# A two-block decoder layer on one core: the order of the delta rule's steps and the engines of its small operations

## The chip, the cores and the metric

The kernel runs on one core of a Trainium2 chip. The core has five engines that work side by side, each through its own instructions in order: TensorE (PE; its weight loads are shown apart as PEld), VectorE (DVE), ScalarE (ACT), GpSimd (POOL) and SyncE (SP), which here only issues DMAs. The metric is the device time of one execution, in microseconds (us), as the median of several runs.

## The reference

Two transformer blocks over one sequence of 256 tokens, width 1024, in float32. The first has two mixers side by side, forgetting attention and a gated delta rule, whose outputs are gated, added and projected, and an MLP with squared ReLU; the second has a SwiGLU, a token mixer and another SwiGLU. What the change touches is the delta rule, with 8 heads of width 128 and chunks of 64 tokens, and a detail of the MLP:

```python
def first_block(x, ...):
    u = rmsnorm(x, norm_mix_g[l])
    proj = u @ w_in[l]
    ...
    qkv = jax.nn.silu(causal_depthwise_conv(jnp.concatenate([gq, gk, gv], axis=-1), gdn_conv_w[l]))
    ...
    o_a = gated_delta_rule_chunked(qh, kh, vh, g, beta).transpose(0, 2, 1, 3)
    o_a = rmsnorm(o_a, gdn_norm_g[l]) * jax.nn.silu(z)
    ...
    x = h + jnp.square(jax.nn.relu(hn @ w_up[l])) @ w_down[l]

def gated_delta_rule_chunked(q, k, v, g, beta):
    ...
    kk = jnp.einsum('bhncd,bhnsd->bhncs', k, k)
    a_mat = jnp.where(tri_strict, beta[..., None] * kk * decay, 0.0)
    rhs = jnp.concatenate([v * beta[..., None], k * (beta * jnp.exp(G))[..., None]], axis=-1)
    sol = lax.linalg.triangular_solve(a_full, rhs, left_side=True, lower=True, unit_diagonal=True)
    ...
    def step(s, inp):
        v_new = value_c - jnp.einsum('bhcd,bhde->bhce', kcum_c, s)
        o = (jnp.einsum('bhcd,bhde->bhce', qdec_c, s)
             + jnp.einsum('bhcs,bhse->bhce', attn_c, v_new))
        s = s * dec_c[..., None, None] + jnp.einsum('bhcd,bhce->bhde', kdec_c, v_new)
        return s, o
```

## The kernel before

**Main line.** The matrix products of both blocks follow each other as one long row of products for TensorE, here called main products: a 128x128 piece of a weight against 256 tokens. `Feed` streams the weights: SP fetches 2048 columns at a time into `raw` (L203, three buffers), ScalarE casts 1024 of them to `wh` (L220), VectorE subtracts to get the rest `wl` (L221), and each piece is used in three products (L258 to L260; L349 to L351 in the projections of the first block's end). A pair `wh`, `wl` feeds 24 main products. Products over 256 columns follow each other at 0.11 to 0.12 us.

**Side lines.** Everything else, norms, attention, the delta rule, runs in generators that `Lines` steps between main products: each `yield pe, wait` says how much TensorE time a stage took and how long, by estimate, until the next may follow. A scheduler then fixes one order for each engine. The order is static: an instruction that is not ready holds everything behind it on its engine.

**The delta rule.** The 8 heads are worked in four groups of two, and two groups form a `Pair` (groups 0 and 1, then 2 and 3). `gdn_group` does for each group:

- the decays: a row DMA on GpSimd's queue with a mask (`rows_everywhere`, L619, L621), exponentials on ScalarE (L755);
- the products of k with k and q (L766); VectorE makes from them `bm`, the matrix to be solved (L780), and `at` (L783);
- `pair.load`: `bm` is written to DRAM as an image (L685) and its diagonal blocks come back (`blk`, L693), both on SP's queue, in order with the `raw` loads;
- `rsqrt_cols` on GpSimd: a bit trick and three Newton rounds on four columns (L146 to L154), then the factor of v (L790);
- the transposes of v and their scaling into `vt` (L798, L801 by way of L170 on ScalarE), then transposes of q and k with squares and scalings (L810 to L816);
- the solution. When both groups of a pair are loaded, `Pair.solve` runs 31 steps of forward substitution on GpSimd for all blocks (L709, L713) and writes to `solved` in DRAM (L716). Each group then fetches its half (`packed` in the tile `xp`, L824, a DMA of GpSimd's queue) and spreads it over four 32-column blocks of `tt` (L833, two on ScalarE, two on VectorE);
- products that finish the inverse (`pp` L849, `pu` L856) and the recurrence (L871 to L911, `apply`), with short VectorE and ScalarE steps between; `HOP` is the wait given between them;
- the output's norm: squares on ScalarE (L919), the sum and the root on GpSimd (L923, `rsqrt_cols`), the scaling of `bm` (by way of L170), the final transposes (L932).

L170 is the helper `scale_rows`, so rows of it are told apart by their tiles. The end of the last two groups falls into the projections of the first block, whose `gate` additions run on GpSimd (L1153). Later, in the MLP, `operand` lays out the second product's operands `ah` and `al` with 4 and 60 unused columns in front (L1174, L1175); the SwiGLUs use 0.

## Time and profile before

| what | us |
|---|---|
| median of 3 runs (lowest, highest) | 1048.19 (1047.76, 1049.74) |
| the profiled execution's own time | 1044.6 |
| its span in the profile | 1042.8 |
| TensorE busy in it | 1005.7 |
| VectorE busy | 673.5 |
| ScalarE busy | 557.0 |
| GpSimd busy | 262.6 |

The profile shows one execution, instruction by instruction; its times count from the start of the span. A row of a timeline gives an instruction's start, its length, its line and operation, its tiles, and in brackets how long the engine had been idle before it and what ended that. The granted clock is TensorE's, as a share of 2.4 GHz: 1.00 is the upper level, 0.50 the lower, 1.2 GHz. Some records of products are missing from a trace, a few in a hundred at most.

### The profile page before, as it was taken

What the parts mean: (1) busy time and instruction counts of PE and PEld (TensorE: products, weight loads), DVE (VectorE), ACT (ScalarE), POOL (GpSimd) and SP (SyncE); (2) the same over time, 40 slices, a digit from 0 to 9 for tenths busy, and PEclk for the clock granted to TensorE, in tenths of its full rate; (3) what the DMA queues carried; (4) which work ended last, traced back from release to release, by engine and by line L of the source; (5) the groups of instructions that cost most, each with busy time, mean ns of one, the idle gap of its engine ahead of it and who ended that gap; (6) DMA issues with size and microseconds to landing.
All of it is one profiled execution on the core that took longest, in us unless ns stands there. A gap on an engine that the chain in (4) does not pass through costs nothing. (4 is left out here: it accounts for less than half of the span.)

```text
span 1042.8 us, 20129 instructions
## 1 busy us (share of the span) xinstructions
PE 1005.7 (96%) x8126; PEld 976.3 (94%) x8126; DVE 673.5 (65%) x1070; ACT 557.0 (53%) x1000; POOL 262.6 (25%) x509
## 2 busy tenths in 40 slices
PE   8999999699797999999999999999999999999997
PEld 7888999699797999999999999999989899999996
DVE  6676898475474787664555666576775687666453
ACT  6766766254634556554444444445576755444542
POOL 1358167638405110000010211140004511121000
PEclk9999999899898999999999999999999999999998
DMA  8656366454342365555455555467644445554551
GB/s 292 242 169 216 123 187 183 146 157 148 92 147 97 119 215 192 183 182 200 167 200 169 196 178 186 152 215 232 220 154 162 163 133 212 187 197 165 167 191 45
DMA packets 39117, 181.93 MB, mean 174 GB/s; under 512 B 11936, under 2 KB 14128, under 8 KB 21232
## 3 DMA queue, kind: packets, MB, share of 16 engines
q1 hardware_dynamic: 37344, 174.85, 48.6%
q0 software_dynamic: 1248, 5.27, 1.9%
q8 instruction: 63, 1.03, 0.4%
q10 hardware_dynamic: 432, 0.53, 0.1%
q14 instruction: 30, 0.25, 0.1%
HBM read 178.25 MB, written 2.38 MB: 173 GB/s over the span
## 5 line engine op out<-in xcount | busy, mean ns | idle before, releaser
L221 DVE TENSOR_TENSOR wl<-raw,wh 128x1024 fp32r<-128x1024 f32 (+2 forms) x347 | 418.2, 1209 | 230.7 <-ACT wh L220 219.7
L220 ACT CAST wh<-raw 128x1024 fp32r<-128x1024 f32 (+2 forms) x347 | 343.8, 996 | 339.4 <-PE g L259 300.6
L259 PE MATMUL g<-Bl,wh 128*128 128x256 f32 x816 | 227.5, 279 | 0.0
L260 PE MATMUL g<-Bh,wl 128*128 128x256 f32 x816 | 227.1, 279 | 0.0
L258 PE MATMUL g<-Bh,wh 128*128 128x256 f32 x816 | 226.9, 279 | 0.0
L258 PE MATMUL g<-Ah,wh 128*128 128x256 f32 x776 | 219.5, 284 | 0.3 <-DVE fnat L994 0.3
L260 PE MATMUL g<-Ah,wl 128*128 128x256 f32 x776 | 219.7, 284 | 0.0
L259 PE MATMUL g<-Al,wh 128*128 128x256 f32 x776 | 218.9, 283 | 0.0
L260 PE MATMUL g<-ah,wl 128*128 128x256 f32 x608 | 170.4, 280 | 0.7 <-DVE wl L221 0.7
L258 PE MATMUL g<-ah,wh 128*128 128x256 f32 x608 | 170.6, 281 | 0.0
L259 PE MATMUL g<-al,wh 128*128 128x256 f32 x608 | 170.6, 281 | 0.0
L258 PEld LDWEIGHTS g<-Bh,wh 128*128 128x128 f32 x816 | 154.3, 190 | 0.0
L260 PEld LDWEIGHTS g<-Bh,wl 128*128 128x128 f32 x816 | 153.3, 188 | 0.0
L259 PEld LDWEIGHTS g<-Bl,wh 128*128 128x128 f32 x816 | 153.3, 188 | 0.0
L258 PEld LDWEIGHTS g<-Ah,wh 128*128 128x128 f32 x776 | 147.7, 191 | 0.9 <-DVE fnat L994 0.7
L259 PEld LDWEIGHTS g<-Al,wh 128*128 128x128 f32 x776 | 146.9, 189 | 0.2
L260 PEld LDWEIGHTS g<-Ah,wl 128*128 128x128 f32 x776 | 146.9, 189 | 0.1
L260 PEld LDWEIGHTS g<-ah,wl 128*128 128x128 f32 x608 | 114.8, 189 | 0.9 <-DVE wl L221 0.9
L258 PEld LDWEIGHTS g<-ah,wh 128*128 128x128 f32 x608 | 114.7, 189 | 0.0
L259 PEld LDWEIGHTS g<-al,wh 128*128 128x128 f32 x608 | 114.7, 189 | 0.0
L1211 POOL TENSOR_TENSOR s<-s,row 128x512 f32<-128x512 f32 x22 | 37.7, 1714 | 207.6 <-ACT s L1210 207.6
L427 POOL TENSOR_TENSOR acc<-acc,sq 128x512 f32<-128x512 f32 x10 | 14.1, 1411 | 243.9 <-ACT sq L422 243.9
(323 smaller groups left out, 1413.4 us busy)
## 6 DMA issues: line engine op xcount, KB each, us to landing
raw<-in_w_in_dram SPq DMA_DIRECT2D x44, 1024.0 KB, 4.9
raw<-in_ffn_gu_dram SPq DMA_DIRECT2D x44, 1024.0 KB, 4.8
raw<-in_ffn_dn_dram SPq DMA_DIRECT2D x32, 704.0 KB, 4.1
raw<-in_w_up_dram SPq DMA_DIRECT2D x16, 1024.0 KB, 4.8
raw<-in_w_down_dram SPq DMA_DIRECT2D x16, 1024.0 KB, 4.8
raw<-in_w_out_dram SPq DMA_DIRECT2D x8, 1024.0 KB, 4.8
raw<-in_w_proj_fox_dram SPq DMA_DIRECT2D x4, 1024.0 KB, 4.7
raw<-in_w_proj_gdn_dram SPq DMA_DIRECT2D x4, 1024.0 KB, 4.7
```

Of the source, the lines that this page charges most:

```text
L220: nc.scalar.copy(hi[:, r], raw[:, r])
L221: nc.vector.tensor_tensor(out=lo[:, r], in0=raw[:, r], in1=hi.bitcast(F32)[:, r], op=ALU.subtract)
L258: nc.tensor.matmul(out, lhsT=w_h, rhs=xh[:, k, :], start=(k == 0), stop=False)
L259: nc.tensor.matmul(out, lhsT=w_h, rhs=xl[:, k, :], start=False, stop=False)
L260: nc.tensor.matmul(out, lhsT=w_l, rhs=xh[:, k, :], start=False, stop=(k == nk - 1))
L427: e.tensor_tensor(out=acc, in0=acc, in1=sq, op=ALU.add)
L1211: nc.gpsimd.tensor_tensor(out=s, in0=s, in1=u.row2, op=ALU.mult)
```

## The change

- A new function `gdn_decays` makes the decays of all four groups; it is spawned for each before the groups, and a group takes its decays from there.
- v is transposed and scaled behind the `pu` product instead of before the solution; the transposes of q and k, with squares and scalings, stand behind the spreading of the solution. The squares' unused output goes to `vnew` instead of `uu`.
- `Pair.solve` itself fetches the packed solutions of both groups, right behind the write, into one tile `packed` that takes the buffer of `sol`.
- Two memsets of each group move from GpSimd to VectorE, and so do the output's sum and root.
- The waits given to the generators change: `HOP` 2.1 for 2.5, 4 for 3 in the solve, 5.5 for 8 in front of the final transposes.
- `ah` and `al` start at offset 0.

```diff
         if jj % 4 == 3:
-            yield 0.0, 3.0
+            yield 0.0, 4.0
         gp.dma_start(out=out.rearrange("a (n i) c -> (a n) (i c)", n=4), in_=sol.rearrange("p i c -> p (i c)"))
+        yield 0.0, 4.0
         self.solved = True
-        yield 0.0, 6.0
+
+        self.packed = g.gx.tile([P, 2, P], F32, tag="sol", name=nm(g, "packed"))
+        for par in range(2):
+            gp.dma_start(
+                out=self.packed[:, par].rearrange("p (a c) -> p a c", c=8),
+                in_=out[16 * par : 16 * par + 16].rearrange("a p c -> p a c"),
+            )
+        yield 0.0, 7.0
         self.done = True
+
+def gdn_decays(g, grp):
+    par, h0 = grp % 2, 2 * grp
+    dec = g.gx.tile([P, 4, P], F32, tag=f"at{par}", name=nm(g, "at"), bufs=2)
+    rows_everywhere(g, dec.rearrange("p (h c) n -> p h (c n)", h=2), h0, 1, g.con["mgdn"], slice(0, 2))
+    yield 0.0, 7.0
+    ngc = g.ngc[:, h0 : h0 + 2].rearrange("p h c -> p (h c)")
+    for i in range(4):
+        g.nc.scalar.activation(out=dec[:, i], in_=dec[:, i], func=AF.Exp, bias=ngc[:, i : i + 1])
+    g.dec[grp] = dec
+    yield 0.0, 1.0
...
-    HOP = 2.5
+    HOP = 2.1
...
-    while "v" not in have:
-        yield 0.0, 0.3
-    vt = have["v"]
-    pv = bank()
-    for i, (h, c) in enumerate(inst):
-        nc.tensor.transpose(pv[:, i], vt[:, h, c * P : (c + 1) * P], g.ident)
-    vn = vt.rearrange("p h (c n) -> p (h c) n", c=2)
-    for i in range(4):
-        scale_rows(g, vn[:, i], pv[:, i], nkv[:, i : i + 1])
-    yield 0.45, 0.0
...
     while not pair.done:
         yield 0.0, 0.5
-    packed = xp[:, 0]
-    nc.gpsimd.dma_start(
-        out=packed.rearrange("p (a c) -> p a c", c=8), in_=pair.out[16 * par : 16 * par + 16].rearrange("a p c -> p a c")
-    )
-    yield 0.0, 7.0
+    packed = pair.packed[:, par]
...
-    nc.gpsimd.memset(half(xp, 1), 0.0)
-    yield 0.0, 3.5
+    nc.vector.memset(half(xp, 1), 0.0)
+
+    kdn = vnew[:, 1:4:2]
+    pk, pq = bank(), bank()
...
+    yield 0.66, 2.8
...
-    nc.gpsimd.memset(y[up], 0.0)
-    yield 0.9, HOP
+    nc.vector.memset(y[up], 0.0)
+    yield 0.9, 0.0
+
+    while "v" not in have:
+        yield 0.0, 0.3
+    vt = have["v"]
...
+    yield 0.45, HOP
...
-    gp.tensor_tensor(out=so, in0=so, in1=base, op=ALU.add)
-    rsqrt_cols(g, r2, so, f"rsq{par}")
+    nc.vector.tensor_tensor(out=so, in0=so, in1=base, op=ALU.add)
+    rsqrt_cols_on(g, nc.vector, r2, so, f"rsq{par}")
     for i in range(4):
         scale_rows(g, o[:, i], o[:, i], r2[:, i : i + 1])
-    yield 0.0, 8.0
+    yield 0.0, 5.5
...
-        ah = operand(act, nf, 4, "ah", "ah")
-        al = operand(act, nf, 60, "al", "al")
+        ah = operand(act, nf, 0, "ah", "ah")
+        al = operand(act, nf, 0, "al", "al")
```

How the order changes, at three places.

ScalarE before, between two weight casts of group 3's projections; `vt_1658` is v of group 2, `tt_1910` and `tt_1963` the spread solutions of groups 0 and 1:

```order
L220 CAST wh_2462<-raw_2408 128x1024
L170 ACTIVATE cacc_2333<-g_2258,par 128x256
L170 ACTIVATE vt_1658<-w_2426,cl_2089 128x128 x4
L220 CAST wh_2525<-raw_2523 128x1024
...
L220 CAST wh_2587<-raw_2585 128x1024
L1118 ACTIVATE gate_1589<-g_2461 128x512
L170 ACTIVATE tt_1910<-xp_1911,con 128x4x32 x2
L639 ACTIVATE kq_2175<-cacc_2340 128x256
L170 ACTIVATE tt_1963<-xp_1964,con 128x4x32 x2
L220 CAST wh_2659<-raw_2585 128x1024
```

And now; `vnew_1942` and `vnew_1967` take the squares of groups 0 and 1, `vt_966` and `vt_1285` are their v:

```order
L220 CAST wh_2704<-raw_2622 128x1024
L170 ACTIVATE tt_1940<-packed_2498,con 128x4x32 x2
L170 ACTIVATE tt_1965<-packed_2498,con 128x4x32 x2
L842 ACTIVATE vnew_1942,ss_1703<-w_2653 128x128 x4
L842 ACTIVATE vnew_1967,ss_1718<-w_2674 128x128 x3
L170 ACTIVATE vnew_1942<-w_2652,ed 128x128
L842 ACTIVATE vnew_1967,ss_1718<-w_2674 128x128
L220 CAST wh_2754<-raw_2752 128x1024
...
L220 CAST wh_2824<-raw_2752 128x1024
L170 ACTIVATE vt_966<-w_2784,cl_1704 128x128 x4
L170 ACTIVATE vt_1285<-w_2793,cl_1719 128x128 x4
```

The scaling of v left the place between the casts and follows the spreading; the spreading of both groups stands three casts later than before, together with the squares.

VectorE now, where the first pair's solution is spread; `bm_2301` is the matrix of group 3, whose image is the last input of the second solve:

```order
L799 SCALAR_TENSOR_TENSOR bm_2301<-w_2330,cl_2303,at_1617 128x128
L221 TENSOR_TENSOR wl_2705<-raw_2622,wh_2704 128x1024
L823 TENSOR_SCALAR tt_1940<-packed_2498,con 128x4x32
L802 TENSOR_TENSOR at_1617<-w_2330,at_1617 128x128
L799 SCALAR_TENSOR_TENSOR bm_2301<-w_2330,cl_2303,at_1617 128x128
L823 TENSOR_SCALAR tt_1940<-packed_2498,con 128x4x32
L823 TENSOR_SCALAR tt_1965<-packed_2498,con 128x4x32 x2
L802 TENSOR_TENSOR at_1617<-w_2330,at_1617 128x128
```

Before, all of group 3's `bm` stood well behind the spreading, among products of group 0; now its last scaling comes right behind the first `tt`.

GpSimd before, at the end of group 2; `gate` is the first block's gate, `so` and `r` the sum and root of the output's norm:

```order
L1153 TENSOR_TENSOR gate_1590<-gate_1590,zt_3905 128x512
L923 TENSOR_TENSOR so_3697<-so_3697,cl_2089 128x4
L146 TENSOR_SCALAR r_528_3743<-so_3697 128x4
L149 TENSOR_SCALAR rsq_3745<-so_3697 128x4
L151 TENSOR_TENSOR rsq_3745<-r_528_3743 128x4
L1153 TENSOR_TENSOR gate_1590<-gate_1590,zt_3943 128x512
L152 TENSOR_TENSOR rsq_3745<-rsq_3745 128x4
```

And VectorE now, with the same sum and root of group 2:

```order
L221 TENSOR_TENSOR wl_3880<-raw_3847,wh_3879 128x1024
L929 TENSOR_TENSOR bm_1943<-bm_1943,w_3656 128x2x128
L937 TENSOR_TENSOR so_3663<-so_3663,cl_1945 128x4
L146 TENSOR_SCALAR r_524_3703<-so_3663 128x4
L149 TENSOR_SCALAR rsq_3705<-so_3663 128x4
L151 TENSOR_TENSOR rsq_3705<-r_524_3703 128x4
L152 TENSOR_TENSOR rsq_3705<-rsq_3705 128x4
L1162 SCALAR_TENSOR_TENSOR gate_3309<-gate_3309,g_3806 128x512
L153 TENSOR_SCALAR rsq_3705<-rsq_3705 128x4
```

The root left GpSimd, where only the gate additions remain, and stands on VectorE between its weight subtractions. On TensorE the final transposes of groups 2 and 3 stand 64 and 42 main products behind their last product of the recurrence before, 99 to 104 and 102 now.

## Rows read from the trace of the kernel before

**Rows 1.** The page, section 1: busy time, share of the span, instructions by engine.

```profile
PE 1005.7 (96%) x8126; PEld 976.3 (94%) x8126; DVE 673.5 (65%) x1070; ACT 557.0 (53%) x1000; POOL 262.6 (25%) x509
```

**Rows 2.** Slices of 20 us: PE, PEld, DVE, ACT, POOL busy, clock, DMA share, GB/s.

```profile
180.00:200.00 20.00, 11.56 (x98) 11.28 (x97) 10.46 (x21) 7.61 (x16) 15.39 (x53) 0.85 0.33 89
200.00:220.00 20.00, 18.69 (x140) 18.11 (x139) 15.33 (x46) 9.21 (x16) 7.37 (x16) 0.90 0.52 169
...
240.00:260.00 20.00, 20.00 (x177) 20.00 (x176) 9.17 (x15) 9.74 (x29) 16.34 (x45) 1.00 0.45 159
260.00:280.00 20.00, 13.51 (x105) 13.30 (x104) 9.07 (x14) 12.26 (x39) 9.14 (x29) 0.83 0.27 66
...
320.00:340.00 20.00, 13.92 (x91) 12.40 (x90) 7.80 (x10) 9.26 (x26) 13.08 (x33) 0.83 0.27 100
340.00:360.00 20.00, 19.34 (x163) 18.92 (x163) 14.30 (x18) 7.75 (x10) 3.49 (x2) 1.00 0.29 106
```

**Rows 3.** The same table for the three stretches at half clock.

```profile
193.86:204.10 10.24, 4.81 (x18) 4.44 (x19) 6.54 (x14) 5.90 (x12) 6.31 (x17) 0.50 0.62 178
265.54:272.37 6.83, 3.20 (x15) 3.20 (x16) 3.87 (x8) 5.58 (x13) 4.01 (x13) 0.50 0.15 10
330.40:337.22 6.82, 5.32 (x23) 4.73 (x23) 2.63 (x3) 2.20 (x5) 5.14 (x14) 0.50 0.01 4
```

**Rows 4.** Waits of TensorE, 180 to 345: us in total, times, longest.

```profile
PE w L911 <- ACT vnew L170: 6.5, 1, 6.5
```

**Rows 5.** Timeline of ScalarE: start, us, instruction, idle before and its releaser.

```profile
195.24 1.14 ACT L170 ACTIVATE vt<-w,cl 128x128 f32<-128x128 f32 x4 [10.75 <-POOL cl L790]
...
208.47 0.93 ACT L170 ACTIVATE tt<-xp,con 128x128 f32<-128x128 f32 x2 [7.27 <-DMA xp<-solved]
...
336.48 1.28 ACT L170 ACTIVATE bm<-bm,r 128x128 f32<-128x128 f32 x4 [4.20 <-POOL r L154]
```

**Rows 6.** Timeline of TensorE in A.

```profile
199.29 1.65 PE L766 MATMUL w<-kq 128*128 128x256 f32 x3 [8.44 <-DVE kq L640]
```

**Rows 7.** Timeline of GpSimd in A, the write and the fetches.

```profile
196.84 0.65 POOL L716 DMA_DIRECT2D solved<-sol  x1 [0.30 <-POOL sol L713]
200.82 2.32 POOL L824 DMA_DIRECT2D xp<-solved  x2 [3.32 <-DMA solved<-sol]
```

**Rows 8.** Timeline of GpSimd, the second solve's first step, write and fetch.

```profile
230.48 0.24 POOL L709 TENSOR_TENSOR stmp<-blk,sol 128x31 f32<-128x31 f32 x1 [7.73 <-DMA blk<-img]
...
259.88 0.65 POOL L716 DMA_DIRECT2D solved<-sol  x1 [0.30 <-POOL sol L713]
262.52 1.20 POOL L824 DMA_DIRECT2D xp<-solved  x1 [1.99 <-DMA solved<-sol]
```

**Rows 9.** Timeline of GpSimd in C, a gate addition and a root's start.

```profile
315.87 1.26 POOL L1153 TENSOR_TENSOR gate<-gate,zt 128x512 f32<-128x512 f32 x1 [25.52 <-DVE zt L1152]
...
329.81 0.20 POOL L923 TENSOR_TENSOR so<-so,cl 128x4 f32<-128x4 f32 x1 [1.39 <-ACT at L919]
```

**Rows 10.** All instructions of L824, 180 to 280: time from issue to landing.

```profile
DMA to landing us min/median/max: 3.7/5.4/7.6
```

**Rows 11.** TensorE in three stretches: length, busy (instructions), clock, DMA share, GB/s.

```profile
463.00:555.00 92.00, 92.00 (x774) 1.00 0.52 184
570.00:697.00 127.00, 127.00 (x1081) 1.00 0.53 185
...
866.00:990.00 124.00, 124.00 (x1096) 1.00 0.53 182
```

**Rows 12.** Timeline of SP's queue, the last image.

```profile
219.79 0.38 SPq L685 DMA_DIRECT2D img<-bm  x1
```

**Rows 13.** VectorE by line and shape, 160 to 345: busy, mean ns, idle before.

```profile
L221 DVE TENSOR_TENSOR wl<-raw,wh 128x1024 fp32r<-128x1024 f32 x43 | 55.0, 1278 | 37.0 <-ACT wh L220 32.6 <-PE g L260 4.4
...
L777 DVE TENSOR_TENSOR cl<-cl,beta 128x2 f32<-128x2 f32 x4 | 0.8, 212 | 0.0
```

**Rows 14.** Timeline of VectorE in front of C.

```profile
316.00 2.22 DVE L221 TENSOR_TENSOR wl<-raw,wh 128x1024 fp32r<-128x1024 f32 x1 [0.28 <-ACT wh L220]
```

More of the change, by code (lines that the diff above doesn't have):

```diff
@@ L749, in gdn_group @@
     ed = g.ed[:, h0 : h0 + 2]
-    at = dec = buf("at", 2)
-    rows_everywhere(g, dec.rearrange("p (h c) n -> p h (c n)", h=2), h0, 1, g.con["mgdn"], slice(0, 2))
-    yield 0.0, 6.0
-    for i in range(4):
-        nc.scalar.activation(out=dec[:, i], in_=dec[:, i], func=AF.Exp, bias=ngc[:, i : i + 1])
+    while grp not in g.dec:
+        yield 0.0, 0.3
+    at = dec = g.dec[grp]
     bm = buf("bm", 2)
@@ L791, in gdn_group @@
     yield 0.0, 2.0
-    while "v" not in have:
-        yield 0.0, 0.3
-    vt = have["v"]
-    pv = bank()
-    for i, (h, c) in enumerate(inst):
-        nc.tensor.transpose(pv[:, i], vt[:, h, c * P : (c + 1) * P], g.ident)
-    vn = vt.rearrange("p h (c n) -> p (h c) n", c=2)
-    for i in range(4):
-        scale_rows(g, vn[:, i], pv[:, i], nkv[:, i : i + 1])
-    yield 0.45, 0.0
     while pair.before and grp - 2 not in pair.before.passed:
@@ L805, in gdn_group @@
     uu, tt, xp, vnew = (buf(n) for n in ("uu", "tt", "xp", "vnew"))
-    kdn = vnew[:, 1:4:2]
-    pk, pq = bank(), bank()
-    for i, (h, c) in enumerate(inst):
-        nc.tensor.transpose(pq[:, i], kq[:, 1, h, c * P : (c + 1) * P], g.ident)
-    for h in range(2):
-        nc.tensor.transpose(pk[:, h], kq[:, 0, h, 0:P], g.ident)
-    for i in range(4):
-        nc.scalar.activation(out=uu[:, i], in_=pq[:, i], func=AF.Square, accum_out=ss[:, 4 + i : 5 + i])
-    for h in range(2):
-        scale_rows(g, kdn[:, h], pk[:, h], ed[:, h : h + 1])
-    gp.tensor_scalar(out=base, in0=ss[:, 4:8], scalar1=P * EPS, scalar2=4 * P * EPS * EPS, op0=ALU.mult, op1=ALU.add)
-    yield 0.66, 0.0
     while not pair.done:
         yield 0.0, 0.5
-    packed = xp[:, 0]
-    nc.gpsimd.dma_start(
-        out=packed.rearrange("p (a c) -> p a c", c=8), in_=pair.out[16 * par : 16 * par + 16].rearrange("a p c -> p a c")
-    )
-    yield 0.0, 7.0
+    packed = pair.packed[:, par]
     for n in range(4):
@@ L841, in half @@
         return v[:, :, :, side]
-    nc.gpsimd.memset(half(xp, 1), 0.0)
-    yield 0.0, 3.5
+    nc.vector.memset(half(xp, 1), 0.0)
+    kdn = vnew[:, 1:4:2]
+    pk, pq = bank(), bank()
+    for i, (h, c) in enumerate(inst):
+        nc.tensor.transpose(pq[:, i], kq[:, 1, h, c * P : (c + 1) * P], g.ident)
+    for h in range(2):
+        nc.tensor.transpose(pk[:, h], kq[:, 0, h, 0:P], g.ident)
+    for i in range(4):
+        nc.scalar.activation(out=vnew[:, i], in_=pq[:, i], func=AF.Square, accum_out=ss[:, 4 + i : 5 + i])
+    for h in range(2):
+        scale_rows(g, kdn[:, h], pk[:, h], ed[:, h : h + 1])
+    gp.tensor_scalar(out=base, in0=ss[:, 4:8], scalar1=P * EPS, scalar2=4 * P * EPS * EPS, op0=ALU.mult, op1=ALU.add)
+    yield 0.66, 2.8
     mask = g.con["m32"].rearrange("p (n b) -> p n b", b=32)
@@ L859, in gdn_group @@
     y, st = xp[:, 0:2], xp[:, 2:4]
-    nc.gpsimd.memset(y[up], 0.0)
-    yield 0.9, HOP
+    nc.vector.memset(y[up], 0.0)
+    yield 0.9, 0.0
+    while "v" not in have:
+        yield 0.0, 0.3
+    vt = have["v"]
+    pv = bank()
+    for i, (h, c) in enumerate(inst):
+        nc.tensor.transpose(pv[:, i], vt[:, h, c * P : (c + 1) * P], g.ident)
+    vn = vt.rearrange("p h (c n) -> p (h c) n", c=2)
+    for i in range(4):
+        scale_rows(g, vn[:, i], pv[:, i], nkv[:, i : i + 1])
+    yield 0.45, HOP
     o = bm
@@ L1101, in first_block @@
         gates = [gp.tile([P, 4, T], F32, tag=f"gate{w}", name=f"gate{w}") for w in range(3)]
+        g.dec = {}
+        for i in range(4):
+            ln.spawn(gdn_decays(g, i), 0.4 * i)
         pairs = [Pair(g)]
```

## The prediction

> **What bounds the kernel now.** I read the page first: TensorE is busy 1005.7 us of a span of 1042.8 [rows 1], so 37 us are idle. The change edits the delta rule, so I cut the stretch that holds it into slices of 20 us [rows 2]: from 240 to 260 TensorE is never idle, but from 180 to 220 it is busy 30.25 of 40 (**idle 9.75**), from 260 to 280 13.51 of 20 (**6.49**), from 320 to 360 33.26 of 40 (**6.74**). That is 23 us in three places, call them A, B and C. In each the granted clock then stands at 0.50, the lower level of 1.2 GHz, after TensorE had been idle, and the 4.81, 3.20 and 5.32 us of work done there [rows 3] would have taken half at the upper level: another 2.4, 1.6 and 2.7. **The most that these stops can give back is 23.0 + 6.7 = 29.7 us.**
>
> Next the waits: TensorE's longest in B is L911 for ScalarE's `vnew` (6.5) [rows 4]. What ScalarE itself waited for, its rows say [rows 5]: the scaling of `vt` 10.75 us for GpSimd's factor, the spreading of the packed solution (`tt`) 7.27 for a DMA, the output's scaling (`bm`) 4.20 for GpSimd's root `r`. ScalarE works in order and also casts every weight tile, so each of these waits holds the weights too, and VectorE's convolution, for which TensorE's L766 waits 8.44 us in A [rows 6].
>
> Then the chain of a solution: written at 196.84 and fetched from 200.82 on in A [rows 7]; the second solve starts at 230.48, writes at 259.88, fetches at 262.52 [rows 8]. In C a root starts on GpSimd at 329.81 [rows 9], and the scaling that needs it at 336.48 [rows 5]: 6.7 us, with gate additions between its steps.
>
> **The change, part by part.**
>
> *Stop A.* `vt` is scaled behind the solution now, and group 2's root enters the solve earlier, so the wait of 10.75 goes. What is late next is `tt`: on ScalarE and VectorE both groups' spreading now stands in front of the next casts. The solve itself gets no shorter (the same steps and the same root), so I leave its write at 196.84 and the first fetch at 200.82; the two issues take 2.32 together [rows 7], and each landing 3.7 to 7.6 us [rows 10]. I take the middle, 5.6, since raw loads are under way then: 206.5 and 207.7. TensorE gets as far as L766 at 199.29 - 8.44 = 190.85 [rows 6], and from there 118 main products at 0.113 [rows 11] lie ahead of the first that needs `tt`: 204.2. (The transposes that leave the stretch before and the products inserted in this one nearly cancel.) With 0.9 for the spreading [rows 5] it goes on at 208.6. **Idle 4.4, between 2.5 and 6.4**, and 1.8 at the lower clock, as B and A cost today. A: 12.2 becomes 6.2, saves 6.0.
>
> *Stop B.* The second solve's input hangs on the first fetch now: on VectorE the last scaling of group 3's `bm` stands behind group 0's `tt`, so its image cannot be written before 206.5 + 0.9 = 207.4. From the image's issue to the first step the trace shows 10.7 us (219.79 to 230.48 [rows 8, 12]): start 218.1. Steps up to the write 29.4, to the fetch 2.6 [rows 8], the second issue 1.2, landing 3.7 (the short one, for the feed stands still then [rows 10]), the last spreads and one scaling on ScalarE 1.4 [rows 5]: ready at 256.4. TensorE has 226 main and 62 inserted products up to there, the latter two records each, so 350 records; a slice without idle holds 177 in 20 us [rows 2]: 39.5 us from 208.6, so it arrives at 248.1. **Idle 8.3**, 2 at the lower clock, and 1 because ScalarE then has the work of two groups at once; between 4 (image out earlier) and 13 (landing 7.6) in all idle. B: 8.1 becomes 11.3, loses 3.2.
>
> *Stop C.* The roots go to VectorE, 15 small operations each. None of 4 columns is in the trace there; the nearest, of 2 columns, takes 212 ns [rows 13]: 3.2 us against 6.7 on GpSimd. The final transposes stand 99 to 104 main products behind the recurrence's last one instead of 42 to 64, which is 11.2 to 11.8 us at 0.113; a root, four scalings (1.28 [rows 5]) and two weight subtractions between (1.28 each [rows 13]) are some 7.1. Left 2, between 0 and 6.7. C: 9.4 becomes 2, saves 7.4.
>
> *The down projection of the MLP.* Its 92 us hold 774 records, 118.9 ns each, another stretch 1081 in 127 (117.5) and a third 1096 in 124 (113.1) [rows 11]; only this stage's operands start at offsets 4 and 60. At offset 0 I expect the nearer rhythm: 768 x 1.4 ns, **1.1 saved**; ends 0 and 4.5. Why a stretch runs at 117.5 or 113.1 the trace doesn't show; if the last one fell to the slower it would cost 4.8, if the other rose it would give 4.8. I expect neither and leave both to the range.
>
> *Costed at nothing.* The decays: the DMAs and masks of all four groups stand before the first solve already, and the exponentials stay between the same casts or nearly so. Memsets on VectorE (four pairs of short operations): VectorE waits for TensorE's products around them; without that cover their own length would come on top, a part of a us in all. Fewer stages for the generators (HOP, yields): they set the order alone, which is counted above.
>
> **Sum:** 6.0 - 3.2 + 7.4 + 1.1 = 11.3 us. The profiled execution took 1044.6, so 1033.3 in its measure; it lies 3.6 below the median of the runs shown, and off that median, 1048.2, the sum leaves **1036.9 us**.
>
> **A rule weighed.** At 316.00 a weight subtraction on VectorE took 2.22 us [rows 14] where its mean is 1.28 [rows 13], begun just behind a GpSimd addition of 1.26 us at 315.87 [rows 9]: one sat behind the other. The Trainium skill, in "SBUF — State Buffer", section "SBUF: two separate sides", says that the two engines share a port pair as an exclusive lock, held for a whole instruction; this trace agrees. It speaks against roots on VectorE, for by it each of the gate additions near the last roots could hold them; the sum would be that of rival 3.
>
> **The rivals.**
> 1. *The stops nearly close.* Fetches land after 3.7 us, and group 3's image is out before the first `tt`: A 3, B 4, C 0, so 22.7 of the 29.7 come back, with 1.1 to 4.5 from the down projection 1021 to 1024; with nothing left of the stops 1014 to 1017. For it: the short landing was seen [rows 10]. Against: so was the long one, and the place of `bm` in the order. **0.20.**
> 2. *Slower: the second solve starts no earlier than now.* Place: the block loads on SP, queued behind raw loads, which wait for casts, which now stand behind `tt`. Price: a us for each us of start after 218.1; at 230.5, with the long landing, 12.4 + 3.9 + 1 at the lower clock: 1054. It decides from a start at 230 on, from 226.5 with the long landing. For: today's wait of 7.73 for blocks [rows 8]. Against: the raw load ahead of that image needs only a cast that stands before `tt`. **0.08.**
> 3. *The roots on VectorE are held.* Four gate additions of 1.26 us [rows 9] would lengthen the chain in C from 7.1 to 12.1, past the 11.2 that are there, and the subtractions queue behind: C stays at 5 to 9, 1040 to 1044. **0.11.**
> 4. *The change doesn't do what it says.* The wait for `vt` is only replaced by an equal one for `tt`: A stays at 12, 1043; or the offsets have no effect, 1038, with B at its upper bound 1043. **0.11.**
>
> The forecast, with each of A, B and C within its bounds (1030 to 1045), has 0.50.
>
> **How the numbers follow.** 0.2% is 2.1 us, about what can be told from no change. The range, 1023 to 1049, leaves out some two thirds of rival 1, nearly all of rival 2 and a little of the rhythms. Faster: 0.47 of the forecast, 0.20, 0.08 and 0.07 of rivals 1, 3 and 4: 0.82. Slower: rival 2, 0.08. Same: the rest, 0.10.
>
> **What would show it.** `vt` starting without a wait on GpSimd, but `tt` waiting some 8 us near 199 and 10 near 245; the second solve's first step near 218; TensorE idle under 2 us from 320 on; 117.5 ns per product in the down projection. If the second solve starts before 213, or TensorE is idle under 4 us at the second fetch, the term for B was wrong; if a scaling of `bm` still waits over 2 us for `r`, that for C.

## The result and the profile after

The changed kernel took 1042.17 us in the median of 6 runs (1038.31 to 1043.78), the kernel before 1047.97 beside it: a ratio of 0.9936, 95% interval 0.9912 to 0.996. It is faster, by 5.8 us instead of the 11.3 forecast; the time lies inside the range and 5.3 above the forecast. The profiled execution took 1038.45.

The page of the changed kernel, section 1, as [rows 1]:

```profile
span 1036.7 us, 20129 instructions
PE 1001.4 (97%) x8126; PEld 973.8 (94%) x8126; DVE 684.5 (66%) x1138; ACT 557.4 (54%) x1000; POOL 244.1 (24%) x441
```

The span is 6.1 shorter: TensorE is busy 4.3 less and idle 1.8 less. The slices of the changed kernel from 200 on, as [rows 2], its two stretches at half clock, as [rows 3], and the down projection, as [rows 11]:

```profile
200.00:220.00 20.00, 4.23 (x37) 4.02 (x35) 2.46 (x9) 2.46 (x11) 10.88 (x38) 0.74 0.49 141
220.00:240.00 20.00, 19.66 (x146) 19.66 (x147) 9.39 (x16) 10.88 (x31) 12.08 (x35) 0.84 0.34 98
240.00:260.00 20.00, 20.00 (x177) 20.00 (x177) 10.89 (x18) 7.43 (x12) 14.74 (x33) 1.00 0.41 139
260.00:280.00 20.00, 18.26 (x162) 18.09 (x161) 15.13 (x53) 16.89 (x64) 0.42 (x2) 1.00 0.37 111
...
320.00:340.00 20.00, 16.10 (x116) 15.49 (x116) 14.29 (x28) 7.80 (x14) 5.04 (x4) 0.83 0.30 106
340.00:360.00 20.00, 19.29 (x168) 19.00 (x168) 17.03 (x20) 10.65 (x15) 3.13 (x2) 1.00 0.38 133
```

```profile
209.51:226.58 17.07, 6.24 (x29) 6.24 (x30) 6.08 (x13) 7.18 (x27) 6.92 (x23) 0.50 0.53 154
328.98:335.81 6.83, 5.62 (x24) 5.22 (x25) 4.58 (x5) 2.20 (x6) 2.18 (x1) 0.50 0.45 156
463.00:555.00 92.00, 92.00 (x785) 92.00 (x783) 48.38 (x46) 38.02 (x45) 4.53 (x4) 1.00 0.52 184
```

Measured as the prediction measured them, idle plus half of the work at half clock, the stops went as follows. A, 200 to 240: 16.1 + 3.1 = 19.2, and it was 12.2. B, 260 to 280: 1.7, with no stretch at half clock, and it was 8.1. C, 320 to 360: 4.6 + 2.8 = 7.4, and it was 9.4. Together 28.4 against 29.7. **The stops gave back 1.3 of the 10.2 forecast: B and C gave 8.3, and A took 7.0 of it.**

The rest is elsewhere. Following the main products by number, the changed kernel is 4.4 ahead when the stretch of the delta rule ends (the 1681st of L258 to L260 and L349 to L351, at 364.75 against 369.10), gains 1.1 in the down projection and 0.6 after it. The same table from 30 us up to that product, of the changed kernel and of the one before:

```profile
30.00:364.75 334.75, 310.20 (x2388) 297.24 (x2387) 238.93 (x507) 192.69 (x458) 146.29 (x316) 0.96 0.48 158
```

```profile
30.00:369.10 339.10, 313.24 (x2390) 298.32 (x2390) 228.13 (x441) 192.62 (x458) 164.90 (x384) 0.96 0.48 156
```

Idle time falls by 1.3 there (25.9 to 24.6) and busy time by 3.0 for as many products. Of the 3.0 the clock explains 0.7 (11.9 us of work at half clock instead of 13.3); no run tells which products the other 2.3 come from.

### The profile page after: what moved, and what is told of

It reads as the page before. It is cut to its first block, busy times and chain, and to the rows that moved or that the text cites. A ratio compares the mean times of both kernels' runs of the same rounds, so it can differ in the third digit from the quotient of the medians.

```text
span 1036.7 us, 20129 instructions
## 1 busy us (share of the span) xinstructions
PE 1001.4 (97%) x8126; PEld 973.8 (94%) x8126; DVE 684.5 (66%) x1138; ACT 557.4 (54%) x1000; POOL 244.1 (24%) x441
## 4 chain that ended last, share of the span: by engine, by line
PE 84%; POOL 5%; DVE 4%; DMA 4%; issue 1%; ACT 1%; SPq 0%; DVEq 0%; POOLq 0%; ACTq 0%
PE g L259 23%; PE g L260 23%; PE g L258 23%; DVE wl L221 2%; PE g L310 2%; PE g L309 2%; PE g L308 2%; POOL stmp L709 1%; POOL sol L713 1%; PE g L350 1%; PE g L351 1%; PE g L349 1%; DMA packed<-solved 1%; DMA raw<-in_ffn_dn_dram 1%; DMA raw<-in_w_first_dram 1%
## 5 line engine op out<-in xcount | busy, mean ns | idle before, releaser
L260 PE MATMUL g<-Bh,wl 128*128 128x256 f32 x816 | 227.3, 279 | 0.0
L258 PE MATMUL g<-Bh,wh 128*128 128x256 f32 x816 | 227.0, 279 | 0.0
L260 PE MATMUL g<-Ah,wl 128*128 128x256 f32 x776 | 219.7, 284 | 0.0
L258 PE MATMUL g<-Ah,wh 128*128 128x256 f32 x776 | 218.3, 282 | 0.3 <-DVE fnat L1008 0.3
L260 PE MATMUL g<-ah,wl 128*128 128x256 f32 x608 | 170.0, 280 | 0.4 <-DVE wl L221 0.4
L258 PE MATMUL g<-ah,wh 128*128 128x256 f32 x608 | 170.3, 280 | 0.0
L260 PEld LDWEIGHTS g<-Bh,wl 128*128 128x128 f32 x816 | 154.5, 190 | 0.0
L258 PEld LDWEIGHTS g<-Bh,wh 128*128 128x128 f32 x816 | 153.0, 188 | 0.0
L258 PEld LDWEIGHTS g<-Ah,wh 128*128 128x128 f32 x776 | 147.5, 191 | 0.8 <-DVE fnat L1008 0.7
L260 PEld LDWEIGHTS g<-Ah,wl 128*128 128x128 f32 x776 | 146.7, 189 | 0.2
L258 PEld LDWEIGHTS g<-ah,wh 128*128 128x128 f32 x608 | 115.2, 190 | 0.0
L260 PEld LDWEIGHTS g<-ah,wl 128*128 128x128 f32 x608 | 114.6, 189 | 0.6 <-DVE wl L221 0.6
```

The source lines that it names most:

```text
L258: nc.tensor.matmul(out, lhsT=w_h, rhs=xh[:, k, :], start=(k == 0), stop=False)
L260: nc.tensor.matmul(out, lhsT=w_l, rhs=xh[:, k, :], start=False, stop=(k == nk - 1))
```

## What the stops show

The waits of TensorE in the changed kernel from 180 to 345, and ScalarE's wait for the fetches:

```profile
PE w L852 <- ACT vnew L842: 16.1, 1, 16.1
PE g L349 <- ACT Ah L175: 3.2, 1, 3.2
PE w L925 <- issue: 1.7, 1, 1.7
```

```profile
ACT tt L170 <- DMA packed<-solved: 22.5, 2, 18.9
```

The 16.1 are A, the 3.2 C. The 1.7 are B: TensorE stopped at 262.39, when the second `tt` had begun (261.57), at products that read `vnew`, which ScalarE scales from 263.43 on, behind the spreading; the profile itself names no releaser there.

The timeline of GpSimd with the first write and fetches, against [rows 7], and of ScalarE with `tt`:

```profile
205.92 0.65 POOL L716 DMA_DIRECT2D solved<-sol  x1 [0.30 <-POOL sol L713]
209.41 2.31 POOL L722 DMA_DIRECT2D packed<-solved  x2 [2.84 <-DMA solved<-sol]
...
225.80 0.49 POOL L709 TENSOR_TENSOR stmp<-blk,sol 128x31 f32<-128x31 f32 x1 [3.95 <-DMA blk<-img]
```

```profile
217.54 1.73 ACT L170 ACTIVATE tt<-packed,con 128x128 f32<-128x128 f32 x4 [18.86 <-DMA packed<-solved]
...
261.57 1.96 ACT L170 ACTIVATE tt<-packed,con 128x128 f32<-128x128 f32 x4 [3.63 <-DMA packed<-solved]
```

The write comes 9.1 later than before, and `tt` 11 later than the forecast's 206.5. TensorE goes on at 220.34, 2.8 behind the start of `tt`: ScalarE spreads both groups first (1.73), and by the profile TensorE waits for the squares behind them. Rows of SP's queue show both ends of the solve's lateness:

```profile
154.61 0.38 SPq L685 DMA_DIRECT2D img<-bm  x1
...
159.69 2.40 SPq L685 DMA_DIRECT2D img<-bm  x1
...
181.76 5.62 SPq L203 DMA_DIRECT2D raw<-in_w_in_dram  x2
205.37 1.91 SPq L693 DMA_DIRECT2D blk<-img  x4
207.38 0.90 SPq L203 DMA_DIRECT2D raw<-in_w_in_dram  x2
218.35 0.38 SPq L685 DMA_DIRECT2D img<-bm  x1
```

The images of groups 0 and 1 leave at 154.61 and 159.69 (150.33 and 154.67 before), so the first step is at 170.71 (164.88), and the steps take 35.2 up to the write (32.0). At 205.37 group 2's block loads go out: they wait for the first solve, whose buffer they reuse, and two weight loads stand behind them on the queue, on which nothing left between 187.4 and 205.37. These then move together with the fetch, as the DMAs from 204 to 218 show (last column: median us from issue to landing):

```profile
raw<-in_w_in_dram SPq DMA_DIRECT2D x2, 1024.0 KB, 8.2
solved<-sol POOLq DMA_DIRECT2D x1, 128.0 KB, 3.2
packed<-solved POOLq DMA_DIRECT2D x2, 64.0 KB, 7.8
```

The first fetch of the kernel before met two weight loads as well (issued at 198.30 and 200.40), and its 7.65 from issue [rows 7] to `tt` [rows 5] is nearly the same.

In C, a gate addition on GpSimd, and VectorE's timeline around group 2's and group 3's roots (the first runs from 314.03 to 323.27, the second from the sum at 317.29 to 328.8; each is 15 operations of 0.15 to 0.17 us where nothing holds them):

```profile
318.42 1.29 POOL L1170 TENSOR_TENSOR gate<-gate,zt 128x512 f32<-128x512 f32 x1 [46.06 <-DVE rsq L153]
```

```profile
318.45 1.28 DVE L154 TENSOR_TENSOR r<-r,rsq 128x4 f32<-128x4 f32 x1
...
325.59 1.27 DVE L152 TENSOR_TENSOR rsq<-rsq 128x4 f32<-128x4 f32 x1
326.79 1.21 DVE L221 TENSOR_TENSOR wl<-raw,wh 128x1024 fp32r<-128x1024 f32 x1
327.92 0.15 DVE L153 TENSOR_SCALAR rsq<-rsq 128x4 f32<-128x4 f32 x1
327.99 0.74 DVE L948 SCALAR_TENSOR_TENSOR zg<-w,gz,zg 128x512 f32<-128x512 f32 x1
```

ScalarE's wait for the roots there:

```profile
ACT bm L170 <- DVE r L154: 2.0, 1, 2.0
```

TensorE does not wait for a scaling of `bm` here: group 2's root ends at 323.27, and its final transposes run from 324.14 to 325.34 without a stop in front of them. It stops behind them, from 326.29 to 329.44, for the operand `Ah` of the projection, which ScalarE casts from `zg`. That product of VectorE (L948) reads the transposes and began 2.65 after them, behind a held step of group 3's root and a weight subtraction.

## The experiments

All ratios are to the kernel before; the changed kernel's is 0.9936. "tt" is the start of the two spreadings; idle is the time between TensorE's records beyond one product, in A, B and C, a slightly wider count than that of the slices. `tt` and idle are of the one profiled execution, which can lie up to 5 us off the kernel's median (the changed kernel's 3.7 below, e5's 3.8 below, e12's 4.7 above). And each edit lets the scheduler fix a new order for every engine, so a run shows what an edit does with the order that follows from it.

| kernel | ratio (95%) | tt, us | idle A / B / C |
|---|---|---|---|
| before | 1 | 208.5, 266.3 | 10.9 / 6.6 / 7.6 |
| changed | 0.9936 (0.9912-0.996) | 217.5, 261.6 | 16.2 / 1.9 / 5.1 |
| e1 | 0.9901 (0.9882-0.992) | 217.0, 261.9 | 14.2 / 4.0 / 3.0 |
| e2 | 0.9952 (0.9937-0.9967) | 211.4, 261.5 | 13.1 / 4.1 / 5.6 |
| e3 | 0.9997 (0.9974-1.0019) | 218.2, 262.4 | 18.2 / 2.6 / 5.6 |
| e4 | 0.9986 (0.9974-0.9998) | 215.0, 257.0 | 12.1 / 6.1 / 7.1 |
| e5 | 1.0006 (0.9989-1.0023) | 210.2, 265.9 | 14.2 / 6.7 / 7.1 |
| e6 | 0.9916 (0.9888-0.9943) | 211.4, 263.3 | 12.4 / 7.4 / 3.0 |
| e7 | 0.9971 (0.9956-0.9986) | 205.8, 262.0 | 10.3 / 6.5 / 6.8 |
| e8 | 0.995 (0.9935-0.9966) | 217.7, 262.2 | 15.4 / 1.8 / 5.2 |
| e9 | 0.989 (0.9863-0.9918) | 214.2, 258.0 | 8.5 / 4.8 / 4.8 |
| e10 | 0.9951 (0.9933-0.9968) | 218.9, 263.3 | 16.9 / 1.9 / 4.1 |
| e11 | 0.9931 (0.9907-0.9955) | 217.5, 262.2 | 15.6 / 2.5 / 2.7 |
| e12 | 0.992 (0.99-0.9939) | 216.9, 259.7 | 10.6 / 2.9 / 7.4 |

### Why the first solution comes late: e1, e3, e5

**e1**, group 2's factor of v on VectorE, so that the first solve's steps on GpSimd have one root less between them:

```diff
-    rsqrt_cols(g, r, sk, f"rsq{par}")
+    re = nc.vector if grp == 2 else gp
+    rsqrt_cols_on(g, re, r, sk, f"rsq{par}")
```

> The changed kernel with one edit: the root of group 2's key norms and the factor of v that is made of it run on VectorE instead of between the steps of the first solve on GpSimd. Theory (stop A is set by the end of the first solve, which the root inside it lengthens): the solve, 35.2 us in the changed kernel, comes near the second one's 28.5, so 30 or less; the first fetch is issued some 5 us before 209.4, TensorE's idle time near 205 to 220 falls from 16.4 to 10 to 12, and the second stop reopens by 1 to 4 us, since TensorE comes there earlier; in all 2 to 5 us less than the changed kernel. Rival (stop A is set by the order of ScalarE's own work in front of the spreading of the solution): the solve gets shorter, but TensorE's idle time at A stays within 1 us of 16.4 and the time with it.

The steps took 33.3 instead of 35.2 (30 or less was expected), but began 1.2 later, so the fetch moved by only 0.5. The interval overlaps the changed kernel's. The root costs the solve some 2 us, and is not what makes it late.

**e3**, `at` of both chunks multiplied behind both scalings of `bm` instead of between them:

```diff
+        for c in range(2):
+            i = 2 * h + c
             nc.vector.tensor_tensor(out=at[:, i], in0=pq[:, c, 1], in1=dec[:, i], op=ALU.mult)
```

> The changed kernel with one edit: the products of the attention block of a head are written behind all scalings of the key rows of that head instead of between them, so that the image that the solve reads is written earlier. Theory (stop A goes back to the late images: those of the groups were written 4.3 to 5 us later than in the kernel before, and the first solve began 5.8 us later, at 170.7): the first step comes 1 to 4 us before 170.7, the fetch as much before 209.4, and the idle time at A falls by as much from 16.4. Rival (the blocks wait for the raw loads ahead of them on SyncE's queue, whenever the images are written): first step within 1 us of 170.7 and no change of the time.

The images left at 153.99 and 160.04, the first step came at 171.49: the edit did not bring them forward, so the run says nothing on what an earlier solve is worth. But its interval does not touch the changed kernel's: with two products moved a few places, the order that followed cost the whole gain. In the profiled execution A is 2 longer, and TensorE is at half clock for 34.1 us instead of 23.9; why was not followed up.

**e5**, one of the two clearings back on GpSimd:

```diff
-    nc.vector.memset(half(xp, 1), 0.0)
+    gp.memset(half(xp, 1), 0.0)
```

> The changed kernel with one line undone: the clearing of half of xp (one short memset for each group) is on GpSimd again, as in the kernel before. By the order of instructions this moves the cast of the next weight tile behind the exponentials of group 0's decays on ScalarE, and on VectorE the low halves of the weights that stand between the scalings of bm for groups 0 and 1 go behind most of them. Theory (stop A is late because the first solve starts late, and that comes of this line, which the prediction costed at a part of a us): the images of groups 0 and 1, written at 154.6 and 159.7 in the changed kernel, come 3 to 5 us earlier, the first step near 165 to 167 instead of 170.7, the fetch near 204 to 206 instead of 209.4, idle time at A 11 to 13 instead of 16.4; part of it is given back at the second fetch, so 2 to 5 us less in all. Rival (the start of the solve depends on the raw loads that stand ahead of the blocks on SyncE's queue): the images come earlier, but the first step stays within 1.5 us of 170.7 and the time within 1 us.

SP's queue and TensorE's waits in e5:

```profile
150.87 0.38 SPq L685 DMA_DIRECT2D img<-bm  x1
...
155.21 0.43 SPq L685 DMA_DIRECT2D img<-bm  x1
...
197.97 1.91 SPq L693 DMA_DIRECT2D blk<-img  x4
199.98 18.12 SPq L203 DMA_DIRECT2D raw<-in_w_in_dram  x3
```

```profile
PE w L838 <- DVE cl L795: 14.0, 1, 14.0
PE w L838 <- ACT bm L170: 6.6, 1, 6.6
```

This one line delayed the solve: with it undone the images leave 3.7 and 4.5 earlier, the first step is at 164.31, 6.4 earlier, and the write at 198.52, 7.4 earlier. In the order of instructions the clearing itself is nothing; moving it shifts group 0's exponentials and scalings of `bm` against the weight casts and subtractions. But the theory on the time fell: A lost only 2 of its 16.2, because behind `tt` (210.2) the factor `cl` stood until 217.9 on VectorE behind the stream transposes, the convolution and two weight subtractions, and B and C opened again. The intervals do not touch: with the line undone and the solve earlier, the kernel is slower than the changed one and no faster than the one before.

### What the fetch waits for: e2, e6, e7

**e2**, the two fetches issued by ScalarE:

```diff
-            gp.dma_start(
+            nc.scalar.dma_start(
```

> The changed kernel with one edit: the packed solutions are fetched by DMAs that ScalarE issues, instead of GpSimd. In the changed kernel the first fetch was issued at 209.4 (3.5 us behind the solution's last write) and landed 8.1 us later. Theory (the queue by which the fetch goes is what takes long): the landing falls under 4 us and the issue follows the write within 1 us, so stop A falls by 4 to 7 us and the time by 2 to 6. Rival (the transfer is slow whatever the queue, since raw loads are under way): landing 6 to 8 us, time within 1 us of the changed kernel. Second rival (ScalarE's casts now stand behind its own wait for the solution): weights come later, TensorE goes idle before 204 for want of them, and the time is 2 us or more above the changed kernel.

The landing shrank to 4.7 to 5.6, with one weight load beside it instead of two, and `tt` came 6.1 earlier. TensorE then waited 12.9 for the same `cl` as in e5. The time is not shown to differ from the changed kernel's.

**e6**, group 2's blocks loaded into a place of their own, so that they need not wait for the first solve and nothing is queued behind them:

```diff
-        while self.before and not self.before.solved:
-            yield 0.0, 0.5
...
+        pairs[1].blk = zg[:, 4:8].rearrange("p a (b c) -> p (a b) c", c=32)
...
+                if i == 2:
+                    ln.finish(pairs[1].side)
```

> The changed kernel with one edit: the blocks of the second pair get a place of their own (in the half of zg that is not yet written then) instead of the buffer that the first solve reads, so that their loads, which stand on SyncE's queue ahead of two loads of weights, no longer wait for the end of the first solve. In the changed kernel these weight loads were held from 187.1 to 207.4 and then ran at the same time as the first fetch of the packed solutions, which landed 8.1 us after its issue. Theory (that collision is a term of stop A): both weight loads are issued before 200, the fetch lands 3 to 5 us after its issue, TensorE's idle time at A falls from 16.4 by 3 to 5 us, and the time by 2 to 5. Rival (the fetch is slow by itself, its pieces being small): it lands after 7 to 8 us again, and the time stays within 1 us.

The DMAs from 195 to 222 in e6:

```profile
solved<-sol POOLq DMA_DIRECT2D x1, 128.0 KB, 2.1
packed<-solved POOLq DMA_DIRECT2D x2, 64.0 KB, 3.9
```

With the blocks and the weight loads let go earlier (187.6 and 194.1) nothing moves beside the fetch, and it lands in 3.9 instead of 7.8. So the transfers beside it cost 4 us. The other runs agree: beside two weight loads the first fetch took 7.6 to 8.1 (before, changed, e1, e3, e5, e8, e10, e11), beside one 4.7 (e2) and 6.0 (e4), beside none 3.9 to 4.2 (e6, e7, e9); but weight loads are not all of it, for in e12 it took 5.9 beside group 3's blocks alone. A gave 3.8, B took 5.5, C gave 2.1; the interval overlaps the changed kernel's.

**e7**, e5 and e6 together:

> The two edits before together: clearing of xp on GpSimd and a place of its own for the second pair's blocks. If both terms are real and independent, the first fetch is issued near 204 to 206 and lands 3 to 5 us later, idle time at A 7 to 10 us instead of 16.4; the second stop then opens to 4 to 8 us, since the second solve starts from group 3's image, which stands behind the first spreading, and TensorE comes there earlier; in all 4 to 9 us less than the changed kernel. If the second solve takes the place of the first as the limit, the gain at A is given back there to within 2 us of the better of the two single edits.

`tt` at 205.8, as forecast for the changed kernel (206.5), and A still idle 10.3: TensorE waits 10.2 for `cl` again. With the second solve where it was (225.8), B stays open at 6.5. Of the 4 to 9 us expected nothing is shown in the time.

### The second solve and the order behind it: e4, e9, e12

**e4**, the transposes and scaling of v back in front of the solution:

```diff
+    while "v" not in have:
+        yield 0.0, 0.3
...
     while pair.before and grp - 2 not in pair.before.passed:
...
-    yield 0.45, HOP
+    yield 0.9, HOP
```

> The changed kernel with one part of the change undone: v is transposed and scaled ahead of the fetch of the solution again, as in the kernel before. Theory (what TensorE waits for at A is the end of the solve, and the scaling's wait for GpSimd's factor was hidden in that): ScalarE waits 5 us or more for the factor again, but the idle time at A stays within 2 us of 16.4 and the time within 2 us of the changed kernel. Rival (moving the scaling behind the solution is what gained): the casts behind the scaling come late, TensorE stops before 200 as in the kernel before, and the time is 4 us or more above the changed kernel.

A fell by 4.1, and B and C opened by 4.2 and 2. Undoing this part alone loses most of the gain of the whole change, and the intervals do not touch: what it gains lies in B and C. Neither expectation had that: A did not stay within 2 us, and TensorE did not stop before 200.

**e9**, every edit that had improved a term: e5, e6, the squares and transposes of q and k ahead of the fetch, the last scaling of group 3's `bm` ahead of the first `tt` (through the mask that `tt` reads), and e10's root. Its core, beside those of e5, e6 and e10:

```diff
+        nc.vector.scalar_tensor_tensor(
+            out=g.col, in0=bm[:, 3, 0:4], scalar=0.0, in1=g.con["blocks"], op0=ALU.mult, op1=ALU.add
+        )
...
-        col = g.con["blocks"][:, n : n + 1]
+        col = (g.con["blocks"] if pair.before else g.col)[:, n : n + 1]
```

> The changed kernel with five edits against the terms found so far: the clearing of xp on GpSimd; a place of its own for the second pair's blocks; the transposes of q and k with their squares ahead of the fetch again, so that TensorE meets nothing at the stop but the spread solution; the spreading tied to group 3's last bm (its column mask is taken over by an operation that reads that bm), so that VectorE writes group 3's image before it waits for the fetch; and a shorter root. Theory (stop A is the landing plus what VectorE has queued behind it, stop B is the second solve, which hangs on group 3's image behind the first spreading): the first spreading near 206, idle time at A 3 to 6 us instead of 16.4; group 3's image before 206 instead of 218.4, the second solve's first step near 212 to 217 instead of 225.8, its spreading near 247 to 253, idle time at B under 5; in all 8 to 14 us less than the changed kernel. Rival (B takes back what A gives, since the second solve is bound by something else, the blocks' loads or GpSimd): second solve not before 222, idle at B 8 us or more, and not over 4 us less in all.

SP's queue in e9, and its DMAs from 195 to 222:

```profile
200.35 0.38 SPq L685 DMA_DIRECT2D img<-bm  x1
201.67 0.33 SPq L203 DMA_DIRECT2D raw<-in_w_in_dram  x1
```

```profile
solved<-sol POOLq DMA_DIRECT2D x1, 128.0 KB, 7.0
packed<-solved POOLq DMA_DIRECT2D x2, 64.0 KB, 4.0
```

Group 3's image leaves at 200.35, 18 us earlier, and the idle time of A and B together falls: 13.3 against 18.1. But the write of 202.64 ran beside the weight load of 201.67 and the block loads from 202.66 on and took 7.0 to land; the fetch went out at 209.93. Each of the three shorter stops still had its stretch at half clock (13.7, 6.8 and 6.8 us; the changed kernel had 17.1 and 6.8).

**e12**, e9 with the v factors of groups 2 and 3 on VectorE and the output roots on GpSimd:

```diff
+    re = nc.vector if grp >= 2 else gp
...
+    gp.tensor_tensor(out=so, in0=so, in1=base, op=ALU.add)
+    rsqrt_cols(g, r2, so, f"rsq{par}")
```

> The kernel of e9 with the roots the other way round: the factors of v of groups 2 and 3 on VectorE, so that GpSimd has none of them between the first solve's steps or ahead of the second solve (in e9 they stood there from 212.3 to 217.6), and the output's roots on GpSimd again, as in e11. Theory (what is left of the stops hangs on GpSimd's queue, and the output's roots are better off there): the first solve takes 34 us or less instead of e9's 36.7 and ends before the weight load that ran into its write in e9 (landing 7.0), so the first spreading comes at 207 to 211 instead of 214.3 and A's idle time is 2 to 5 instead of 8.7; the second solve's first step comes 5 to 9 us before e9's 219.3, idle time at B 0 to 4 instead of 5.0; between 320 and 350 it is 2 to 3 instead of 4.9; in all 5 to 10 us less than e9. Rival (the write and the fetches run into a weight load wherever they fall, and the roots on VectorE hold back the scalings and spreads there): A and B together stay above 10 us of idle time and the time within 2 us of e9.

The write met a weight load again, with group 3's image beside it (landing 6.0), and the fetch (210.99) met group 3's block loads, which leave from 211.36 on (landing 5.9). Its profiled execution took 1042.61 where its median is 1037.96, so its idle times may overstate. Neither e9 nor e12 is shown faster than the changed kernel: their intervals overlap its own, and the 8 to 14 us expected of e9 and the further 5 to 10 of e12 did not come.

### The roots: e8, e10, e11

**e8**, the gate additions moved from GpSimd to VectorE, so that none sits beside a root:

```diff
-            nc.gpsimd.tensor_tensor(out=gt, in0=gt, in1=t, op=ALU.add)
+            nc.vector.tensor_tensor(out=gt, in0=gt, in1=t, op=ALU.add)
```

> The changed kernel with one edit: the additions of the gates in the first half of the output projection, which GpSimd did in the changed kernel, run on VectorE. Theory (the roots of the output, moved to VectorE, are held there while GpSimd adds: four operations of 4 columns took 1.27 to 1.75 us beside such an addition, where others took 0.15): no operation of the roots takes over 0.3 us, TensorE's idle time between 320 and 350 falls from 5.6 us to 2 or less, and the half clock after it goes with it, so 3 to 5 us less in all. Rival (VectorE is busy in its own order there, and the additions on it stand ahead of the roots): the roots are short but start later, idle time stays within 1.5 us of 5.6, and the time within 1 us of the changed kernel or above it.

No operation of a root is held any more, 0.15 to 0.17 us each, yet the second root took 13 us, 318.0 to 331.1, ScalarE waits 2.5 us for a root instead of 2.0, and C's idle time stays. (Of the four held operations that the expectation counts, three are of a root, 1.27 to 1.29; the 1.75 is a subtraction of 512 columns.) The additions hold single operations; what stretches the root is that its 15 dependent steps stand between those of the other root, gate products of 0.69 and subtractions of 1.22.

**e10**, the same root in fewer steps, 11 instead of 15:

```diff
-    rsqrt_cols_on(g, nc.vector, r2, so, f"rsq{par}")
+    rsqrt_cols_short(g, r2, so, f"rsq{par}")
```

> The changed kernel with one edit: the root of the output sums on VectorE takes 11 operations instead of 15, with the same three steps (two of its products are fused with a neighbour). In the changed kernel the second root took from 317.3 to 328.8, its operations alternating with weight subtractions and the other root's. Theory (it is the number of links of the chain, each of which waits for the operation put in between, that stretches the root): the second root takes 7 to 9 us instead of 11.5, idle time between 320 and 350 falls from 5.6 to 3 or less, 2 to 4 us less in all. Rival (the place in VectorE's order is set by what surrounds it): the root ends at the same time to within 1 us, and nothing changes.

It ran 9.2 instead of 11.5, but its sum began later, and it ended at the same 328.9. No gain.

**e11**, sum and root back on GpSimd:

```diff
-    nc.vector.tensor_tensor(out=so, in0=so, in1=base, op=ALU.add)
-    rsqrt_cols_on(g, nc.vector, r2, so, f"rsq{par}")
+    gp.tensor_tensor(out=so, in0=so, in1=base, op=ALU.add)
+    rsqrt_cols(g, r2, so, f"rsq{par}")
```

> The changed kernel with one part of the change undone: the sum and the root of the output are on GpSimd again. Theory (the roots' move did help, though less than the 7.4 us that the prediction gave it): the roots end later than in the changed kernel, ScalarE waits for them 4 us or more, idle time between 320 and 350 is 7 to 10 us instead of 5.6, and the time 2 to 4 us above the changed kernel. Rival (the root on VectorE is stretched to as long as it was on GpSimd): idle time there stays within 1.5 us of 5.6 and the time within 1.5 us.

The slice of C and ScalarE's wait in e11:

```profile
320.00:340.00 20.00, 17.96 (x138) 17.30 (x138) 11.10 (x14) 8.87 (x15) 12.35 (x26) 0.91 0.30 107
```

```profile
ACT bm L170 <- POOL r L154: 4.8, 2, 3.0
```

TensorE is busy 17.96 there against 16.10, and C's idle time halves to 2.7, although the scaling waits longer for the root. So, by this execution, the move of the roots did not give what C gained; it rather cost some 2 us there. That leaves, above all, the later place of the transposes, which was not tried alone. In the whole time it makes no difference that can be told.

## Why the prediction was right and wrong

**Direction and range: right. Size: half, and for the most part not by its steps.** The stops, forecast at 10.2, gave 1.3; of the rest only the 1.1 of the down projection was foreseen. That the sum still came out at half is luck: 2.3 of it came from work that no term named, and B made good what A lost.

*Stop A, 6.2 forecast, 19.2 measured.* The step that failed is "The solve itself gets no shorter ..., so I leave its write at 196.84". Its start came 5.8 later and its steps took 3.2 more. The start is the memset that I costed at "a part of a us in all": true of its length, wrong of the order that it shifts (e5). The landing, 5.6 forecast and bounded by 7.6 [rows 10], was 8.1 from the first issue to `tt`, from the transfers beside it (e6). The middle was the wrong choice: [rows 10] mixes A's fetches with B's, and A's first took the 7.6, beside two weight loads as now. TensorE's arrival was right: 204.2 forecast, its last record before the stop starts at 203.95. And a term was missing: what stands behind `tt`. TensorE went on 2.8 behind its start instead of 0.9, and where `tt` came in time, TensorE still waited 10 us for `cl` (e7). Rival 4 told this stop better: the wait of 10.75 for `vt` was replaced by one of 18.9 for `tt`. Its 1043 is near the measured 1042.17, but with B and C as forecast, so that is luck too.

*Stop B, 11.3 forecast, 1.7 measured.* The mechanism was as told: group 3's image stands behind the first `tt` (218.35 behind 217.54). Only the solve then started 7.5 after it, not 10.7, at 225.8 instead of 218.1, and its steps took 28.5 instead of 29.4. The second `tt` came at 261.57, and TensorE, 14 us later than forecast (its last product before the stop starts at 262.12, against 248.1) because of A, found it under way. By the test the prediction set, idle under 4 at the second fetch, the term was wrong, and mostly because A's was. A and B together were forecast at 17.5 and came to 20.9, 20.3 before. Most runs say why the two can't be read apart: the second `tt` stays at 257 to 266 whatever the first one does, so what an edit gains in A, TensorE waits for in B. The sum of their idle time fell by more than 2 us only in e9 and e12, from 18.1 to 13.3 and 13.5. Both send group 3's image ahead of the first `tt`, but that alone is not the reason: e3 and e4 do so too (208.55 and 207.21), and their sums are 20.8 and 18.2.

*Stop C, 2 forecast, 7.4 measured.* Two steps failed. The price of the root, "takes 212 ns [rows 13]: 3.2 us against 6.7 on GpSimd": the operations are even shorter, but the chains took 9.2 and 11.5. And the end of the chain: the transposes do stand late enough that TensorE does not wait for them, but what follows them, `zg` on VectorE and its cast, had no term, and TensorE's 3.2 are a wait for that. By the sign that the prediction set, a scaling waiting over 2 us for `r`, the term is at the edge: 1.99. Rival 3 gave the right size, C at 5 to 9. Its mechanism is there: the addition above ran from 318.42 to 319.71, and the root's step beside it took 1.28 where 0.15 would do, as in [rows 14]. The Trainium skill, in "SBUF — State Buffer", section "SBUF: two separate sides", calls the port pair of the two engines an exclusive lock, held for a whole instruction; these rows agree. One such step (325.59) even stands in front of `zg`. But e8 shows that the holding does not set C's size: without it C's idle time stays, 5.2 against 5.1. What its timeline leaves is the alternation with other work, and e11, with the roots off VectorE, halves C's idle time.

*Down projection.* 117.2 ns a record (92 / 785) against 117.5 forecast, and 1.1 gained there. The offsets are the one edit to that stage; they were not tried alone.

*The rest.* 2.3 us of less busy time in the delta rule had no term. It was not isolated, nor were the decays and the closer steps tried alone. What is shown of the parts: v behind the solution pays (e4), the clearing on VectorE pays in this order though it delays the solve (e5), the roots on VectorE don't (e11), and which engine issues the fetch makes no difference that is shown (e2). Which part of the change the whole 5.8 us come from stays open beyond that.

## What to carry to other kernels

Where two stops lie on one chain, sum them: a term for the second is worth nothing until the first arrival holds, and an edit that hastens the first alone moves the wait. A short operation moved to another engine is priced not by its length but by what it reorders there: look at the order of instructions before it, back to the chain's start. A chain of n small dependent operations on a busy engine costs what stands between them, not n times its mean; and the operations behind it, up to the engine that must not stop, belong to the sum.

## What the runs showed of the hardware

- With nothing else moving, a write of 128 KB landed in 2.1 us and a fetch of 64 KB in 3.9 (e6). Begun 1 us behind a load of 1 MB, with block loads beside it, the write took 7.0 (e9); begun 1.5 to 2 us behind two loads of 1 MB, the fetches took 7.8 (changed kernel).
- The granted clock fell to 0.50 within the stops of 8.4 us (before, at 193.86) and 16.1 (changed, at 209.51); in B of the changed kernel, 1.7 idle, it stayed at 1.00. Three shorter stops (e9) had 27.3 us at half clock in all, the changed kernel 23.9: less idle time did not mean less time at the low clock.
- On VectorE a 128x4 operation took 1.27 to 1.29 us instead of 0.15 beside a gate addition of GpSimd; with the additions on VectorE none did (e8).
